# Low parts of the attention weights: accumulating DMAs in place of GpSimd's subtractions

## The chip, the cores and the metric

The kernel runs on one core of a Trainium2 chip. A core has engines that run their own instruction queues side by side: TensorE (in the profile PE for matmuls, PEld for weight loads), VectorE (DVE), ScalarE (ACT), GpSimd (POOL) and SyncE (SP, which here only issues DMAs). GpSimd can issue DMAs too, and only those of its queue add to what lies at their destination in this kernel. The metric is the device time of one launch in microseconds, as the median of the runs.

## The reference

Two layers of an encoder for 512 tokens with 1024 channels, in float32. Cut to what matters:

```python
for l in range(DEPTH):                       # 2
    h = rms_norm(x, ln1_g[l])
    proj = h @ w_in[l]                       # split: A's q, k, v; B's q, k, v; C's ranks; gate logits
    y_a = gqa_axial(...)                     # attention A: 8 query heads, 2 key heads
    y_b = diff_attention(...)                # attention B: 8 heads, difference of two softmaxes
    y_c = mla(...)                           # attention C: 8 heads from low-rank latents
    y = stack([y_a, y_b, y_c])
    merged = sum(sigmoid(gate_logits) * (y @ w_branch[l]), over the three)
    x = x + merged @ w_out[l]
    x = x + square(relu(rms_norm(x, ln2_g[l]) @ w_ff1[l])) @ w_ff2[l]
return rms_norm(x, final_g)
```

The kernel multiplies in float32r, a type to which its casts round. To keep the accuracy, each operand is split into a high part (the value rounded to float32r) and a low part (the value minus the high part), and a product is made of three: high by high, high by low, low by high.

## The kernel before

The kernel is written for a tile scheduler: the program lists the operations, and the scheduler makes each engine's order from the order of the list, the data each operation needs, and when a buffer comes free. A list of items, each with a cost in microseconds of TensorE, is the plan (`plan`, from line 1020 on). `run` (line 167) walks it. Before each item it does what has come due: weights whose item starts within `AHEAD_F` are fetched (a DMA of SP's queue into a buffer `wr`), weights whose item starts within `AHEAD_S` are split (`get`, line 55). So these two numbers set where in the list a weight's operations stand.

A weight is a `Weight` (line 43): 128 partitions by 256 to 1024 columns. `get` writes the high part `wh` with ScalarE (line 61, a cast) and the low part `wl` with a subtraction (line 67). There are two buffers of `wr` (`NWR`) and three each of `wh` and `wl` (`NW`). A cast waits until the matmuls of the weight three before have ended, and a fetch until the weight two before has been read for the last time, which is the end of the subtraction.

The subtraction is made by VectorE in one piece, or by GpSimd in pieces of 256 columns. `nw` counts the weights, and of each five those with `nw % 5 < POOLW` go to GpSimd. `POOLW` is `P0` = 1 at a layer's start (its projections), `PA` = 5 from the first attention to the last gates, so that all go to GpSimd there, and `PF` = 0 after that (output projection and MLP). The marked places are lines 1029, 1052, 1066 and 1130.

The order of a layer: keys and values of A, queries of A, parts of B's projections; then attention A woven with the rest of B's projections; attention B woven with gate matmuls (`gate_branch`, line 976) and C's projections; attention C woven with gates and C's per-pair projections; the last gates and branches; the output projection; the MLP. An attention item (`probs`, line 588) makes scores in PSUM (`sc`), their row maximum with VectorE (line 594), the exponential with ScalarE (line 599), the normalised rows with VectorE (lines 604 and, for B, 754 to 756); later the transposes (`pT`, line 610), the copies out of PSUM by ScalarE and VectorE (lines 613, 614) and the products with the values (`pv`).

The MLP's second product multiplies by sums of weight blocks (`Blocks`, line 72). Some of these sums are made by DMAs of GpSimd's queue that add one block onto another (lines 95 and 96). They are not changed.

Of the kernel before, what the change touches and what calls it, by code (L numbers as in the profile page):

```python
# [10 lines left out]
F32 = mybir.dt.float32  # L11
F32R = mybir.dt.float32r
I32 = mybir.dt.int32
AF = mybir.ActivationFunctionType
ALU = mybir.AluOpType
# [27 lines left out]
class Weight:  # L43
# [11 lines left out]
    def get(self):  # L55
        if self.parts is None:
            self.fetch()
            t = self.t
            wh = t.p.tile([128, self.cols], F32R, tag="wh", name="wh", bufs=t.NW)
            wl = t.p.tile([128, self.cols], F32R, tag="wl", name="wl", bufs=t.NW)  # L60
            t.nc.scalar.copy(wh, self.raw)  # L61
            t.nw += 1

            e, n = (t.nc.gpsimd, 256) if t.nw % 5 < t.POOLW else (t.nc.vector, 1024)
            for o in range(0, self.cols, n):
                q = slice(o, min(o + n, self.cols))
                e.tensor_tensor(wl[:, q], self.raw[:, q], wh[:, q].bitcast(F32), op=ALU.subtract)  # L67
            self.parts = wh, wl
        return self.parts

# [71 lines left out]
class Trunk:  # L142
# [24 lines left out]
    def run(self, plan):  # L167

        at, ws = 0.0, []
        for c, _, w in plan:  # L170
            ws += [(at - getattr(x, "lead", 0.0), x) for x in w]
            at += c
        ws.sort(key=lambda x: x[0])
        t0, kf, kg = self.t, 0, 0
        for c, f, _ in plan:
            now = self.t - t0
            while kf < len(ws) and ws[kf][0] <= now + self.AHEAD_F:
                ws[kf][1].fetch()
                kf += 1
            while kg < len(ws) and ws[kg][0] <= now + self.AHEAD_S:  # L180
                ws[kg][1].get()
                kg += 1
            self.tick(self.t)
            f()
            self.t += c

    @staticmethod
    def weave(att, fill):

        tf = sum(x[0] for x in fill)  # L190
        done, k, r = 0.0, 0, []
        for i, a in enumerate(att):
            r.append(a)
            while k < len(fill) and done + fill[k][0] / 2 <= tf * (i + 1) / len(att):
                r.append(fill[k])
                done += fill[k][0]
                k += 1
        return r + fill[k:]
# [821 lines left out]
    def plan(self, l):  # L1020
        nc = self.nc

        def begin():
            self.aG, self.aK, self.aR, self.ys = {}, {}, {}, {"a": {}, "b": {}, "c": {}}
            self.bz = {}
            self.bf, self.bs, self.bV = {"q": {}, "k": {}}, {"q": {}, "k": {}}, {}
            self.cQ, self.cK, self.cV, self.qr, self.mg, self.cf, self.mp, self.gc = {}, {}, {}, {}, {}, {}, {}, {}
            self.layer_consts(l)
            self.POOLW = self.P0
            self.hold = []  # L1030

        def stat():
# [13 lines left out]
        weave = self.weave  # L1046
        kv = self.a_kv(l)
        r = [(0, begin, [])] + kv + [(0, stat, [])] + self.a_q(l, 0) + self.a_q(l, 1)
        fb = self.b_qk(l, "q", 0) + self.b_qk(l, "k", 0) + self.b_v(l, 0)
        fb1 = self.b_qk(l, "q", 1) + self.b_qk(l, "k", 1) + self.b_v(l, 1)  # L1050
        r += fb[: self.FB]
        r += [(0, lambda: setattr(self, "POOLW", self.PA), [])]
        r += weave(self.att_a(), fb[self.FB :] + fb1)
        gb = [[self.gate_branch(l, n, d) for d in range(8)] for n in range(3)]
        att = self.att_b(l)
# [5 lines left out]
        g2 = [x[0] for x in gb[2]]  # L1061
# [1 line left out]
        r += weave(att[8:16], self.c_pair(l, 2) + self.c_v(l, 1) + gates(1, 4, 8))  # L1063
        r += weave(att[16:24], self.c_pair(l, 3) + g2[:3])
        r += weave(att[24:], g2[3:6])
        r += [(0, lambda: setattr(self, "POOLW", self.PF), [])] + g2[6:]
        r += [(0, self.tick, [])] + [x[1] for x in gb[2]]
        xs, x2, st2, ff = [], [], {}, []

# [57 lines left out]
                hs[p] += [h[:, :, 0:256], h[:, :, 256:512]]  # L1127

        def stat2():
            self.POOLW = self.PF  # L1130
            v = self.stat_var(self.stat_join(st2))
            self.r2 = self.p.tile([128, 4], F32, tag="rstd", name="r2", bufs=1)
            self.rsqrt(self.r2, v, 4)
# [71 lines left out]
        for c, n in enumerate(CHUNKS):  # L1205
            for j in range(2 * n):
                w = self.big(l, P_FF1 + j0 + j)
                if c and j < 2:
                    w.tag = "pt"
                r.append((cost, lambda j=j, w=w: ff1(j, w), [w]))  # L1210
                if c == 0 and j < 2:
                    r.append((0, rbc2 if j else stat2, []))
            j0 += 2 * n
            for m in range(4):
                blocks = Blocks(self, self.ff2_blocks(l, c, m), n)
                f = {i: Factor(blocks, i, 3.0 if m == 0 else 1.5) for i in range(1, 8)}
                order = [(i, (0, n)) for i in (1, 4, 2, 6, 5, 7, 3)]
                if m == 0:

                    e = n - 2  # L1220
                    order = [(1, (0, n))] + [(i, (0, e)) for i in (2, 4, 5)] + [(i, (e, n)) for i in (2, 4)]
                    order += [(6, (0, n)), (5, (e, n)), (7, (0, n)), (3, (0, n))]
                if c + 1 == len(CHUNKS) and l + 1 == self.depth and m == 3:
                    order = [(i, (0, n)) for i in (1, 4, 2, 6, 7, 5, 3)]
                for i, part in order:
                    r.append(((part[1] - part[0]) * 0.36, lambda c=c, m=m, i=i, w=f[i], part=part: ff2(c, m, i, w, part), [f[i]]))
# [12 lines left out]
    def go(self):  # L1239
        tc, nc = self.tc, self.nc  # L1240
        self.t, self.due, self.hold, self.nb, self.nw = 0.0, [], None, 0, 0

        self.NS4, self.NWR, self.NW, self.NTMP, self.NP = 25, 2, 3, 4, 4
        self.BANKS = {"S": 2, "T": 2, "V": 1, "L": 3}

        self.AHEAD_F, self.AHEAD_S = 8.0, 3.0
        self.LAG_T, self.LAG_V, self.LAG_C = 5.5, 6.0, 9.0
        self.LAG_Q, self.LAG_KV, self.LAG_R = 14.0, 14.0, 60.0

        self.P0, self.PA, self.PF = 1, 5, 0  # L1250
        self.FB = 16
        self.TAGQ = "ST"
        self.POOLW = self.P0
        with tc.tile_pool(name="c", bufs=1) as self.c, tc.tile_pool(name="p", bufs=1) as self.p, \
                tc.tile_pool(name="pp", bufs=1, space=bass.MemoryType.PSUM) as self.pp, \
                tc.tile_pool(name="pd", bufs=1, space=bass.MemoryType.DRAM) as pd:
            self.xd = pd.tile([128, 8, 512], F32, name="xd") if self.depth > 1 else None
            self.st, self.xg, self.xs = {}, [None] * 8, []
            plan = sum((self.plan(l) for l in range(self.depth)), [])
            self.setup()  # L1260
            self.g = self.c.tile([128, self.a["gains"].shape[1]], F32, name="g")
            nc.sync.dma_start(self.g, self.a["gains"])
            for d in range(8):
                if d % 2 == 0:
                    x = self.s4("x", dtype=F32)
                nc.sync.dma_start(x[:, d % 2], self.a["xT"][:, d])
                self.xs.append(x[:, d % 2])
                if d in (0, 4):
                    plan[1 + 3 * (d // 4)][2][0].fetch()
            self.tables()  # L1270
            for d in range(8):
                self.first_norm(0, d)
                if d in (0, 4):
                    plan[1 + 3 * (d // 4)][2][0].get()
            for d in range(8):
                self.stat_add(self.st, d, self.xs[d])
            self.run(plan)
# [108 lines left out]
```

## Time and profile before

| what | value |
|---|---|
| median of 3 runs (lowest, highest) | 1873.94 us (1873.64, 1875.34) |
| the profiled execution | 1873.65 us, its span 1871.9 us |
| TensorE busy | 1820.1 us, 97% |
| VectorE busy | 1382.5 us, 74% |
| ScalarE busy | 1010.6 us, 54% |
| GpSimd busy | 473.8 us, 25% |
| GpSimd's low parts (line 67) | 402 pieces, 296.4 us |
| granted TensorE clock | 0.994 |

The span runs from the first to the last instruction of the profiled execution. A group of instructions is told as line, engine, operation, what it writes and reads, and how many; then its busy time, the mean duration of one in ns, the idle time of the engine just before them, and what ended most of it. A row of the waits is who waited, for whom, us in total, times, and the longest. A row of the timeline is start, duration, engine, line, operation, and in brackets the idle time before it. The attentions fill about 75 to 525 us in the first layer and 985 to 1465 us in the second.

### The profile page before, as it was taken

To read this page: it belongs to the slowest core of one execution; us is meant where nothing else is said; L and a number is where in the kernel's file an instruction comes from. 1 tells how busy PE (TensorE), PEld (TensorE's weight loads), DVE (VectorE), ACT (ScalarE), POOL (GpSimd) and SP (SyncE) were. 2 spreads that over 40 slices of the span, in tenths; PEclk is the share of its full clock that TensorE was granted. 3 is DMA by queue.
4 is the path that set the end of the run, shared out by engine and by line. 5 is a ranking of instruction groups with operands and counts; after the bars stand their busy time and mean duration, and the time that the engine had idled before them with its cause. 6 is when DMAs were issued, how large, how long until landed. Compare 5 with 4: busy or idle time off the path is not lost.

```text
span 1871.9 us, 30054 instructions
## 1 busy us (share of the span) xinstructions
PE 1820.1 (97%) x10960; PEld 1601.4 (86%) x10960; DVE 1382.5 (74%) x2815; ACT 1010.6 (54%) x1852; POOL 473.8 (25%) x622
## 2 busy tenths in 40 slices
PE   8999999999999999999999999999999999999997
PEld 8998878777888898988999988788878888989897
DVE  8788889755665776767887888796566667777677
ACT  5577666655544544444545766665554444444443
POOL 4321443454101110101243224434540001001011
PEclk9999999999999999999999999999999999999998
DMA  5213341332143373645632134313232525637353
GB/s 163 69 51 86 96 108 48 96 84 81 51 169 101 93 184 103 155 130 133 153 104 64 41 101 113 93 49 89 81 93 65 166 90 118 168 95 183 106 145 95
DMA packets 85059, 197.26 MB, mean 105 GB/s; under 512 B 11952, under 2 KB 28720, under 8 KB 84912
## 3 DMA queue, kind: packets, MB, share of 16 engines
q1 hardware_dynamic: 74544, 178.56, 31.9%
q0 software_dynamic: 10368, 16.78, 6.0%
q8 instruction: 87, 1.43, 0.3%
q14 instruction: 60, 0.49, 0.1%
HBM read 174.32 MB, written 4.19 MB: 95 GB/s over the span
## 4 chain that ended last, share of the span: by engine, by line
PE 74%; DVE 11%; DMA 6%; ACT 5%; issue 2%; POOL 1%; SPq 0%; DVEq 0%; ACTq 0%; POOLq 0%
PE ff L222 18%; PE ff L1162 13%; PE gate L222 12%; PE br L222 6%; PE tm L314 5%; PE out L222 4%; PE sc L222 4%; PE pv L222 4%; PE pT L610 3%; DMA fa<-wff 2%; DMA wr<-w 2%; PE c_rank L222 2%; DVE mx L594 1%; DVE p L756 1%; DVE fl L116 1%
## 5 line engine op out<-in xcount | busy, mean ns | idle before, releaser
L67 POOL TENSOR_TENSOR wl<-wr,wh 128x256 fp32r<-128x256 f32 (+1 forms) x402 | 296.4, 766 | 533.2 <-ACT wh L61 512.0
L61 ACT CAST wh<-wr 128x1024 fp32r<-128x1024 f32 (+5 forms) x246 | 224.6, 914 | 343.8 <-PE ff L222 113.7
L1162 PE MATMUL ff<-h,fh 128*128 128x256 f32 x1792 | 324.4, 283 | 2.1 <-DVE x L1170 1.8
L222 PE MATMUL ff<-xg,wh 128*128 128x512 f32 x1024 | 315.8, 390 | 0.0
L1162 PEld LDWEIGHTS ff<-h,fh 128*128 128x128 f32 x1792 | 279.0, 192 | 4.2 <-issue 2.5
L1162 PE MATMUL ff<-h,fl 128*128 128x256 f32 x896 | 254.2, 285 | 1.9 <-DVE fl L116 1.8
L222 PE MATMUL gate<-xg,wh 128*128 128x512 f32 x768 | 241.9, 393 | 1.1 <-DVE c_K L230 1.1
L222 PEld LDWEIGHTS ff<-xg,wh 128*128 128x128 f32 x1024 | 191.7, 188 | 39.5
L115 ACT CAST fh<-fa 128x640 fp32r<-128x640 f32 (+1 forms) x144 | 108.8, 762 | 177.8 <-PE ff L1162 100.0
L314 PE MATMUL tm<-wh,xg 128*128 128x256 f32 x1024 | 203.4, 290 | 0.0
L594 DVE TENSOR_REDUCE mx<-sc 128x1 f32<-128x512 f32 x256 | 173.8, 683 | 38.4 <-PE sc L222 37.4
L222 PE MATMUL ff<-xg,wl 128*128 128x512 f32 x512 | 199.2, 389 | 0.0
L1162 PEld LDWEIGHTS ff<-h,fl 128*128 128x128 f32 x896 | 171.1, 192 | 5.3 <-DVE fl L116 4.8
L222 PEld LDWEIGHTS gate<-xg,wh 128*128 128x128 f32 x768 | 142.9, 188 | 29.9 <-PE pv L222 1.4
L314 PEld LDWEIGHTS tm<-wh,xg 128*128 128x128 f32 x1024 | 165.6, 193 | 0.2
L116 DVE TENSOR_TENSOR fl<-fa,fh 128x640 fp32r<-128x640 f32 (+1 forms) x144 | 126.3, 881 | 36.9 <-ACT fh L115 33.9
L67 DVE TENSOR_TENSOR wl<-wr,wh 128x1024 fp32r<-128x1024 f32 (+3 forms) x117 | 134.1, 1146 | 25.8 <-ACT wh L61 25.8
L222 PE MATMUL gate<-xg,wl 128*128 128x512 f32 x384 | 150.6, 392 | 0.0
L613 ACT CAST pt<-pT 128x512 fp32r<-128x512 f32 x192 | 111.8, 585 | 65.0 <-PE pT L610 62.9
L314 PE MATMUL tm<-wl,xg 128*128 128x256 f32 x512 | 145.7, 285 | 0.0
L614 DVE TENSOR_TENSOR pt<-pT,pt 128x512 fp32r<-128x512 f32 x192 | 131.3, 686 | 19.3 <-ACT pt L613 17.7
L96 POOL DMA_DIRECT2D fa<-wff x24 | 21.5, 896 | 421.8 <-DMA fa<-wff 302.4
(253 smaller groups left out, 3610.4 us busy)
## 6 DMA issues: line engine op xcount, KB each, us to landing
wr<-w SPq DMA_DIRECT2D x170, 512.0 KB, 3.6
fa<-wff SPq DMA_DIRECT2D x64, 320.0 KB, 3.5
wr<-w SPq DMA_DIRECT2D x52, 256.0 KB, 2.9
fa<-wff SPq DMA_DIRECT2D x32, 384.0 KB, 3.8
b_sq<-b_f SPq DMA_DIRECT2D x96, 64.0 KB, 2.9
b_sk<-b_f SPq DMA_DIRECT2D x96, 64.0 KB, 2.0
fa<-wff POOLq DMA_DIRECT2D x16, 320.0 KB, 4.8
fs<-wff SPq DMA_DIRECT2D x32, 160.0 KB, 2.7
```

The source lines that it names most:

```text
L61: t.nc.scalar.copy(wh, self.raw)
L67: e.tensor_tensor(wl[:, q], self.raw[:, q], wh[:, q].bitcast(F32), op=ALU.subtract)
L96: t.nc.gpsimd.dma_start(r["21"], self.src[0], accum_op=ALU.add)
L115: t.nc.scalar.copy(a, x)
L116: t.nc.vector.tensor_tensor(b, x, a.bitcast(F32), op=ALU.subtract)
L222: self.nc.tensor.matmul(out, l, r, start=(i == 0), stop=(i == n - 1))
L314: self.nc.tensor.matmul(ps, l, r, start=(u == 0 and i == 0 and tt % 2 == 0), stop=(u == 1 and tt % 2 == 1 and i == len(p) - 1))
L594: nc.vector.tensor_reduce(m, s, axis=AX.X, op=ALU.max, negate=True)
L610: nc.tensor.transpose(T[:, k], p[:, k * 128 : (k + 1) * 128], self.ident)
L613: nc.scalar.copy(h[:, :, q], T)
L614: nc.vector.tensor_tensor(lo[:, :, q], T, h[:, :, q].bitcast(F32), op=ALU.subtract)
L1162: nc.tensor.matmul(bk[tag], x, y, start=(new and a == 0), stop=(part[1] == n and a == len(pairs) - 1), skip_group_check=True)
```

## The change

For a weight that GpSimd split, ScalarE now writes two tiles: the high part as before, and minus the high part, into the low part's buffer. Then a DMA on GpSimd's queue reads the weight from HBM once more and adds it there, so that the low part stands in the buffer when the DMA has landed. VectorE's subtraction is no longer cut at 1024 columns; no weight is wider than that. The variable is renamed to `DMAW`, with the same values at the same places. While it isn't zero, weights are split 6.0 ahead (`AHEAD_D`) and not 3.0; fetches are made 10.0 ahead and not 8.0, everywhere.

```diff
             t.nc.scalar.copy(wh, self.raw)
             t.nw += 1
-            e, n = (t.nc.gpsimd, 256) if t.nw % 5 < t.POOLW else (t.nc.vector, 1024)
-            for o in range(0, self.cols, n):
-                q = slice(o, min(o + n, self.cols))
-                e.tensor_tensor(wl[:, q], self.raw[:, q], wh[:, q].bitcast(F32), op=ALU.subtract)
+            if t.nw % 5 < t.DMAW:
+                t.nc.scalar.activation(wl, self.raw, AF.Copy, scale=-1.0)
+                t.nc.gpsimd.dma_start(wl, self.src, accum_op=ALU.add)
+            else:
+                t.nc.vector.tensor_tensor(wl, self.raw, wh.bitcast(F32), op=ALU.subtract)
             self.parts = wh, wl
...
-            while kg < len(ws) and ws[kg][0] <= now + self.AHEAD_S:
+            while kg < len(ws) and ws[kg][0] <= now + (self.AHEAD_D if self.DMAW else self.AHEAD_S):
                 ws[kg][1].get()
...
-        self.AHEAD_F, self.AHEAD_S = 8.0, 3.0
+        self.AHEAD_F, self.AHEAD_S, self.AHEAD_D = 10.0, 3.0, 6.0
...
-        self.POOLW = self.P0
+        self.DMAW = self.P0
```

More of the change, by code (lines that the diff above doesn't have):

```diff
@@ L1051, in plan @@
         r += fb[: self.FB]
-        r += [(0, lambda: setattr(self, "POOLW", self.PA), [])]
+        r += [(0, lambda: setattr(self, "DMAW", self.PA), [])]
         r += weave(self.att_a(), fb[self.FB :] + fb1)
@@ L1065, in plan @@
         r += weave(att[24:], g2[3:6])
-        r += [(0, lambda: setattr(self, "POOLW", self.PF), [])] + g2[6:]
+        r += [(0, lambda: setattr(self, "DMAW", self.PF), [])] + g2[6:]
         r += [(0, self.tick, [])] + [x[1] for x in gb[2]]
@@ L1129, in stat2 @@
         def stat2():
-            self.POOLW = self.PF
+            self.DMAW = self.PF
             v = self.stat_var(self.stat_join(st2))
@@ L1252, in go @@
         self.TAGQ = "ST"
-        self.POOLW = self.P0
+        self.DMAW = self.P0
         with tc.tile_pool(name="c", bufs=1) as self.c, tc.tile_pool(name="p", bufs=1) as self.p, \
```

## Prediction

> **What bounds the kernel now.** I read the first page from the top: span, busy times, then the chain that ended last.
>
> ```profile
> span 1871.9 us, 30054 instructions
> PE 1820.1 (97%) x10960; PEld 1601.4 (86%) x10960; DVE 1382.5 (74%) x2815; ACT 1010.6 (54%) x1852; POOL 473.8 (25%) x622
> ...
> PE 74%; DVE 11%; DMA 6%; ACT 5%; issue 2%; POOL 1%; SPq 0%; DVEq 0%; ACTq 0%; POOLq 0%
> ```
>
> TensorE is busy for 97% of the span, and GpSimd, whose work the change takes away, makes 1% of the chain. Next come the two stretches of the attentions, one in each layer (busy times by window; the columns are the stretch, then PE, PEld, DVE, ACT, POOL with their counts, clock, DMA share and GB/s).
>
> ```profile
> 75.00:525.00 450.00, 438.81 (x2555) 374.57 (x2554) 338.12 (x762) 283.35 (x581) 159.18 (x216) 1.00 0.28 77
> 985.00:1465.00 480.00, 467.17 (x2721) 399.68 (x2721) 363.77 (x809) 297.90 (x604) 163.69 (x222) 1.00 0.28 80
> ```
>
> Here TensorE is idle for 450.00 - 438.81 = 11.2 us and 480.00 - 467.17 = 12.8 us. These 24.0 us are nearly all that any change to the helpers of the attentions can win, about 1.3% of the span. VectorE is at 75%, ScalarE at 63%.
>
> Who is waited for in them? First, the low part's own line over the whole span (who waited for line 67), then TensorE's longest waits in the first stretch.
>
> ```profile
> who waited for it (us, times):
> ...
>   PEld tm L327: 0.3, 1
>   PEld tm L314: 0.2, 1
> ```
>
> ```profile
> PE pT L610 <- DVE p L604: 3.2, 3, 2.7
> ```
>
> ```profile
> PEld sc L222 <- ACT p L599: 7.1, 17, 1.6
> ```
>
> TensorE waited 0.5 us in all for a low part. What it waits for in the attentions is the softmax: ScalarE's exponential (a score bank comes free) and VectorE's normalised rows. So making the low parts sooner is worth nothing by itself; the change can win only through VectorE and ScalarE, and lose by late low parts.
>
> **What is removed.** GpSimd's subtractions, and with them their hold on VectorE.
>
> ```profile
> L67 POOL TENSOR_TENSOR wl<-wr,wh 128x256 fp32r<-128x256 f32 (+1 forms) x402 | 296.4, 766 | 533.2 <-ACT wh L61 512.0
> L61 ACT CAST wh<-wr 128x1024 fp32r<-128x1024 f32 (+5 forms) x246 | 224.6, 914 | 343.8 <-PE ff L222 113.7
> ...
> L67 DVE TENSOR_TENSOR wl<-wr,wh 128x1024 fp32r<-128x1024 f32 (+3 forms) x117 | 134.1, 1146 | 25.8 <-ACT wh L61 25.8
> ```
>
> There are 246 high parts and 117 low parts on VectorE, so GpSimd makes 129, in 402 pieces of 296.4 us. GpSimd is on no path here, so those us are free; what counts is VectorE beside it. The trace has one plain case (in order of time), and then the two rows of line 756 (least, median and greatest ns; then busy us and mean ns):
>
> ```profile
> 231.41 0.15 DVE L254 TENSOR_TENSOR rst<-rst,rsh 128x8 f32<-128x8 f32 x1
> ...
> 231.84 1.32 DVE L756 SCALAR_TENSOR_TENSOR p<-p,z 128x512 f32<-128x512 f32 x1
> ...
> 231.88 4.65 POOL L67 TENSOR_TENSOR wl<-wr,wh 128x256 fp32r<-128x256 f32 x6 [6.41 <-ACT wh L61]
> ...
> 233.09 0.71 DVE L256 TENSOR_TENSOR rst<-rsy 128x8 f32<-128x8 f32 x1
> ...
> 236.65 0.50 PE L222 MATMUL sc<-b_sk,b_sq 96*128 96x512 f32 x1 [1.17 <-ACT p L599]
> ```
>
> ```profile
> L756 DVE SCALAR_TENSOR_TENSOR p<-p,z x64: 734/752/1323, 179.8 to 1260.3; 128x512 f32<-128x512 f32 x64
> ```
>
> ```profile
> L756 DVE SCALAR_TENSOR_TENSOR p<-p,z 128x512 f32<-128x512 f32 x64 | 55.3, 864 | 0.9
> ```
>
> While GpSimd runs its six pieces, an operation of 0.15 us takes 0.71 and line 756 takes 1.32; TensorE then waits 1.17 us. Line 756 has a median of 752 ns and a mean of 864, so its 64 instructions lose 64 x 0.112 = 7.2 us of VectorE, half of it in each layer. How much of this is on the path? The least is nothing, the most is the 24.0 us of idle time; the one wait of 1.17 us is shown, others are likelier small. I take 3 us a layer, **-6 us**, with 0 and -15 as bounds (no reason lets all idle time go, since the waits for ScalarE stay).
>
> **What is added on ScalarE.** 129 passes that write minus the high part. The trace has no such pass; the nearest row is the cast of the same tile on the same engine, in the first stretch:
>
> ```profile
> L61 ACT CAST wh<-wr 128x1024 fp32r<-128x1024 f32 (+3 forms) x65 | 54.0, 833 | 65.2 <-PE gate L222 29.6 <-issue 18.6 <-DMA wr<-w 10.6
> ```
>
> 129 x 0.833 = 107 us, about 54 a layer, which lifts ScalarE in the first stretch from 283 to 337 of 450 us, 75%. Behind each pass on ScalarE's queue stand the exponentials and the copies of the transposed probabilities, and TensorE waits for these. If its 7.1 us of waits for the exponential grow with the load (337/283), that is +1.3 us a layer; where a pass of 1.05 us falls just ahead of a wait, it is added whole. One such place is known:
>
> ```profile
> 461.36 0.41 PE L610 MATMUL pT<-ident,p 128*128 128x128 f32 x2 [2.69 <-DVE p L604]
> ```
>
> Together 2 us a layer, **+4 us**. Bounds: 0 (ScalarE has 167 us of idle time there), and +17, if each of the 17 waits becomes 0.5 us longer in both layers.
>
> **What is moved: the low part's landing.** It now needs the second pass, then a DMA of GpSimd's queue that reads the weight again and adds. The trace has such DMAs in the MLP:
>
> ```profile
> q1 hardware_dynamic: 74544, 178.56, 31.9%
> q0 software_dynamic: 10368, 16.78, 6.0%
> ...
> wr<-w SPq DMA_DIRECT2D x170, 512.0 KB, 3.6
> ...
> fs<-wff POOLq DMA_DIRECT2D x32, 160.0 KB, 4.5
> fa<-wff POOLq DMA_DIRECT2D x8, 384.0 KB, 5.0
> ```
>
> From 160 to 384 KB the time from issue to landing grows by 0.5 us, so I estimate 5.3 us for 512 KB, the issue itself included. From the end of the cast to the low part: 1.05 + 5.3 = 6.35 us, where GpSimd needs four pieces of 0.766 = 3.1. So each is 3.3 us later. Does TensorE notice? Four weights in order of time: the cast, GpSimd's pieces, the first matmul that reads the low part.
>
> ```profile
> 23.81 1.05 ACT L61 CAST wh<-wr 128x1024 fp32r<-128x1024 f32 x1 [1.63 <-DMA wr<-w]
> ...
> 29.02 0.28 PE L314 MATMUL tm<-wl,xg 128*128 128x256 f32 x1
> ```
>
> ```profile
> 186.50 1.05 ACT L61 CAST wh<-wr 128x1024 fp32r<-128x1024 f32 x1
> ...
> 197.65 0.40 PE L222 MATMUL gate<-xg,wl 128*128 128x512 f32 x1
> ```
>
> ```profile
> 340.63 1.05 ACT L61 CAST wh<-wr 128x1024 fp32r<-128x1024 f32 x1
> ...
> 341.76 4.27 POOL L67 TENSOR_TENSOR wl<-wr,wh 128x256 fp32r<-128x256 f32 x6 [5.30 <-ACT wh L61]
> ...
> 345.25 0.39 PE L222 MATMUL gate<-xg,wl 128*128 128x512 f32 x1
> ```
>
> ```profile
> 364.25 0.73 POOL L67 TENSOR_TENSOR wl<-wr,wh 128x256 fp32r<-128x256 f32 x1 [8.48 <-ACT wh L61]
> ...
> 368.75 0.39 PE L222 MATMUL gate<-xg,wl 128*128 128x512 f32 x1
> ```
>
> The cast at 186.50 is the usual case: it ends at 187.55, the new low part lands at 193.9, and the matmul comes at 197.65, so 3.7 us are left. The tight ones: 341.68 + 6.35 = 348.0 against 345.25, 2.8 us late; 364.2 (GpSimd starts right behind the cast) + 6.35 = 370.5 against 368.75, 1.8 late; 24.86 + 6.35 = 31.2 against 29.02, 2.2 late. With the first two in each layer: 2 x 4.6 + 2.2 = 11.4 us, if nothing else changes. Three things do. The weight's buffer comes free at the end of the second pass (342.7), not of GpSimd's fourth piece (344.6), so the fetch of the weight after next is issued 1.9 us earlier; SP's queue shows that it waits for just that:
>
> ```profile
> SPq L53 <- POOL wl L67: 299.2, 120, 8.4
> ```
>
> The longer lookahead (6.0 for 3.0) asks for a weight earlier, ahead of the attention's items on ScalarE. And the order of TensorE's matmuls is made anew by the scheduler, which puts other ready work ahead of a late part. I keep about a third, **+4 us**; bounds 0 and +23 (twice 11.4, if the landings take longer than in the MLP).
>
> Weighed against the Trainium skill: "DMA: Bandwidth & Descriptors", section "Anatomy of one DMA — SWDGE (gpsimd) path", fits such a DMA with about 2.0 us plus its bytes at 436 GB/s, and by it 512 KB would take 3.2 us, the low part would come only 1.2 us later than now, and this term would be about nothing (an estimate from that page). The rows of this trace, 4.5 us already for 160 KB, disagree, and the sum goes by them.
>
> **The rest.** What an issue costs GpSimd, from the MLP:
>
> ```profile
> L96 POOL DMA_DIRECT2D fa<-wff x24: 857/862/1426, 630.8 to 1839.0; - x24
> ```
>
> It issues 129 DMAs at some 0.86 us for 402 pieces, so its own queue gets shorter; the sums of squares and the merged branches that stand behind them wait no longer than now. The added traffic is 402 pieces of 128 KB, 52.7 MB. At the queue's price (6.0% of 1871.9 us for 16.78 MB, 6.7 us a MB) that is 353 us of all 16 engines, over 930 us: the share rises from 0.28 to 0.66. That is below full, and I cost it at nothing; if not, the second rival prices it. Fetching 10.0 ahead and not 8.0 finds SP's queue held by buffers as now: nothing, within 3 us either way.
>
> **Sum.** -6 + 4 + 4 = +2 us. The profiled execution took 1873.65 us (span 1871.9 and 1.75 around it); the median of the runs is 1873.94, 0.3 above, so the forecast is 1875.7 for such an execution and **1876 us** for a median.
>
> **Rivals.**
> *Relief wins.* VectorE's free port shortens the softmax enough to remove half of the 24.0 us of idle time, and the late parts are hidden: 1874 - 12 + 2 = 1864. For it: the 1.17 us case, and VectorE at 75%. Against: only 7.2 us of line 756 is lost to it.
> *The low parts come late (slower).* One mechanism: accumulating DMAs at a share of 0.66 land as the slowest of the MLP do, 9.1 us in the row below, not 5.3. It decides once a landing takes over 9 us: then the tight weights are late by 6.6, 5.6 and 6.0, so 2 x 12.2 + 6.0 = 30 us; with two thirds of it real, 1894.
>
> ```profile
> DMA to landing us min/median/max: 3.2/4.6/9.1
> ```
>
> The Trainium skill has a rule that would drive this: "SBUF — State Buffer", section "SBUF: two separate sides", says that VectorE's two-port operations keep GpSimd from writing descriptors; no run shows yet what it does here.
> *ScalarE becomes the bound.* The +17 us of its upper bound, less 3 of relief: 1888. For it: 75% load with the exponentials behind; against: 113 us of idle time left.
> *The lookahead alone pays.* Weights asked for earlier remove a third of the idle time, the rest cancels: 1866.
>
> **How the numbers follow.** Forecast (1870 to 1881) 0.40, relief 0.25, ScalarE 0.17, late parts 0.10, lookahead 0.08. Faster, the same and slower are parted at 0.2% (3.7 us), about what a measurement of this kernel can tell. Of the forecast's 0.40 I give 0.04 to faster, 0.24 to the same, 0.12 to slower. Faster: 0.04 + 0.25 + 0.08 = 0.37; slower: 0.12 + 0.17 + 0.10 = 0.39; the same 0.24. The range is 1861 to 1893; it leaves out the ends of relief and of late parts.
>
> **What will show it.** GpSimd's busy time falls by about 185 us (296 less 129 x 0.86); ScalarE's rises by 107; line 756's mean falls from 864 to about 752; issue to landing of the new DMAs at 5.3 us; TensorE's waits for low parts under 5 us a layer. I am wrong if these DMAs land in 4 us or in 8, if ScalarE's exponentials take over TensorE's waits, or if the two stretches' idle time moves by more than 10 us.

## The result and the profile after

| what | before | after |
|---|---|---|
| median of 4 runs (lowest, highest) | 1873.79 us (1871.38, 1875.34) | 1928.20 us (1922.73, 1932.96) |
| ratio, 95% interval | | 1.0292 (1.0276 to 1.0307) |
| the profiled execution, its span | 1873.65, 1871.9 us | 1932.96, 1931.2 us |
| granted TensorE clock | 0.994 | 0.979 |

The change makes the kernel 2.9% slower, where 2 us more had been forecast; 1928 lies 35 us above the upper end of the range. The changed kernel has one line more above most of the functions: line 222 is now 223, line 756 is 757, and so on; line 65 is the new ScalarE pass and line 66 the new DMA.

The first page of the changed kernel: span, busy times, queues, the chain that ended last.

```profile
span 1931.2 us, 29908 instructions
PE 1844.8 (96%) x10960; PEld 1618.8 (84%) x10960; DVE 1348.3 (70%) x2813; ACT 1101.0 (57%) x1983; POOL 288.3 (15%) x351
...
q0 software_dynamic: 29232, 69.92, 22.0%
...
PE 76%; DMA 9%; issue 5%; ACT 5%; DVE 4%; POOL 0%; SPq 0%; ACTq 0%; DVEq 0%; POOLq 0%
```

Of the 59.3 us by which the span grew, 24.7 are TensorE's busy time (1844.8 - 1820.1), with the same 10960 matmuls, and 34.6 its idle time. VectorE is busy for 34 us less and has nearly left the chain (11% to 4%); DMAs grew in it (6% to 9%). The two stretches of the attentions (columns as in the prediction):

```profile
75.00:525.00 450.00, 421.04 (x2409) 358.32 (x2408) 310.09 (x728) 312.21 (x619) 74.22 (x89) 0.97 0.58 129
985.00:1465.00 480.00, 452.95 (x2700) 391.09 (x2699) 338.25 (x800) 327.75 (x651) 87.23 (x110) 0.97 0.57 127
```

Idle time went from 11.2 to 29.0 us in the first and from 12.8 to 27.1 in the second, and the clock, 1.00 in both before, is 0.97. (The stretches are fixed times; as the changed kernel runs behind by up to 59 us, they hold somewhat less of its work.) TensorE's waits (who waited for whom, us, times, longest) say for what:

```profile
PE gate L223 <- DMA wl<-w: 39.9, 14, 5.2
...
PE tm L223 <- DMA wl<-w: 5.0, 2, 2.9
PE tm L315 <- DMA wl<-w: 4.5, 1, 4.5
...
PE tm L328 <- DMA wl<-wkv: 3.4, 1, 3.4
PE uk L223 <- DMA wl<-w: 3.3, 2, 1.7
```

20 waits of 56.1 us together for the low parts' DMAs, where there had been 0.5 us for low parts. The waits for the softmax, which had been the largest of the attentions, have nearly gone (before, then after):

```profile
PE pT L610 <- DVE p L604: 5.7, 5, 2.7
...
PE sc L222 <- ACT p L599: 3.7, 4, 1.2
```

```profile
PE pT L611 <- DVE p L605: 1.0, 2, 0.5
...
PE sc L223 <- ACT p L600: 0.2, 1, 0.2
```

The DMAs themselves, issue to landing in us (DMA issues by size), and what SP's queue waits for ahead of a weight's fetch:

```profile
wr<-w SPq DMA_DIRECT2D x170, 512.0 KB, 3.9
wl<-w POOLq DMA_DIRECT2D x76, 512.0 KB, 7.1
...
wl<-w POOLq DMA_DIRECT2D x36, 256.0 KB, 5.0
...
wl<-w POOLq DMA_DIRECT2D x8, 128.0 KB, 4.0
```

```profile
SPq L53 <- ACT wl L65: 444.5, 90, 13.6
```

A low part of 512 KB lands 7.1 us after its issue, in the median. The last row suggests a cause of part of it, which no run tested by itself: the event that lets the accumulating DMA go, the end of the ScalarE pass, is also the one that lets the fetch of the weight after next go, since that pass is now the last reader of the raw weight. So the two transfers start side by side. The longest wait for a low part, in order of time (start, duration, engine, line):

```profile
245.21 1.08 ACT L65 ACTIVATE wl<-wr 128x1024 fp32r<-128x1024 f32 x1
...
246.31 9.82 SPq L53 DMA_DIRECT2D wr<-w  x3
...
246.58 0.86 POOL L66 DMA_DIRECT2D wl<-w  x1 [7.73 <-ACT wl L65]
...
247.93 0.86 POOL L66 DMA_DIRECT2D wl<-w  x1 [0.49 <-ACT wl L65]
...
257.04 0.80 PE L223 MATMUL gate<-xg,wl 128*128 128x512 f32 x1 [5.20 <-DMA wl<-w]
257.63 1.06 PE L223 MATMUL gate<-xg,wh 128*128 128x512 f32 x2
...
262.33 0.63 PE L223 MATMUL gate<-xg,wl 128*128 128x512 f32 x1
262.75 0.85 PE L223 MATMUL gate<-xg,wh 128*128 128x512 f32 x2
263.44 0.39 PE L223 MATMUL gate<-xg,wl 128*128 128x512 f32 x1
```

The pass ends at 246.29. A fetch goes at 246.31, the first of three, the gate's accumulating DMA at 246.58 and that of the next weight at 247.93; the gate's lands 10.4 us after its issue. Behind the wait of 5.20 us the same matmul takes 0.63 us until 262.33, and 0.39 from 263.44 on. That is the second part of the loss, and the granted clock shows it. Fifteen of the twenty waits last 2 us or more. The windows of 6.1 us behind them follow (the column after POOL is the clock). The first eleven are the gates' waits, of 2.00, 2.40, 2.41, 2.82, 3.19, 3.54, 3.60, 3.70, 4.09, 4.82 and 5.20 us in this order; the last four are those of the time-major products (`tm`), of 2.10, 2.87, 3.41 and 4.48 us:

```profile
1328.60:1334.70 6.10, 6.10 (x25) 5.06 (x26) 1.17 (x3) 0.74 (x2) 0.00 (x0) 0.75 0.25 49
211.90:218.00 6.10, 6.07 (x20) 4.83 (x21) 1.19 (x3) 0.16 (x2) 0.00 (x0) 0.72 1.03 217
1437.20:1443.30 6.10, 6.07 (x20) 4.86 (x21) 2.23 (x5) 4.62 (x8) 0.86 (x1) 0.72 0.68 166
485.70:491.80 6.10, 6.10 (x21) 4.96 (x22) 1.85 (x4) 4.19 (x6) 0.86 (x1) 0.77 0.72 150
1165.60:1171.70 6.10, 6.10 (x15) 4.82 (x16) 0.81 (x2) 0.00 (x0) 0.00 (x0) 0.54 0.99 212
1313.10:1319.20 6.10, 6.09 (x22) 4.96 (x23) 2.63 (x5) 4.55 (x9) 0.68 (x1) 0.72 0.20 74
360.50:366.60 6.10, 6.10 (x18) 4.92 (x19) 2.50 (x5) 3.31 (x7) 0.00 (x0) 0.58 0.24 72
1210.10:1216.20 6.10, 6.06 (x16) 4.76 (x17) 0.00 (x0) 0.28 (x1) 1.82 (x2) 0.55 0.82 175
1346.20:1352.30 6.10, 6.10 (x15) 4.82 (x16) 0.00 (x0) 0.00 (x0) 0.00 (x0) 0.52 0.68 136
393.40:399.50 6.10, 6.05 (x21) 4.93 (x22) 0.00 (x0) 0.00 (x0) 0.00 (x0) 0.76 0.49 99
257.00:263.10 6.10, 6.06 (x14) 4.84 (x15) 0.00 (x0) 0.00 (x0) 0.89 (x1) 0.50 0.71 170
...
1376.80:1382.90 6.10, 5.52 (x32) 4.25 (x32) 3.94 (x8) 4.40 (x10) 0.43 (x1) 1.00 0.80 187
423.40:429.50 6.10, 5.96 (x29) 5.18 (x29) 2.51 (x5) 2.59 (x6) 0.00 (x0) 0.72 0.80 180
970.60:976.70 6.10, 6.08 (x25) 6.08 (x26) 1.22 (x1) 1.04 (x1) 1.03 (x3) 0.51 0.33 126
33.60:39.70 6.10, 6.10 (x35) 6.10 (x36) 5.32 (x18) 0.29 (x1) 1.63 (x4) 0.64 0.32 101
```

One minus the clock, summed over the fifteen, is 5.00; times 6.1 us that is 30.5 us. TensorE's busy time is 24.7 us above that of the kernel before, and 31.3 us above that of the kernel without these DMAs (1813.5 us, below), which has none of these waits. So the lower clock behind the waits accounts for nearly all of the slower matmuls.

### The profile page after: what moved, and what is told of

Its sections match the earlier page's. It is cut to its first block, busy times and chain, and to the rows that moved or that the text cites. A ratio compares the mean times of both kernels' runs of the same rounds, so it can differ in the third digit from the quotient of the medians.

```text
span 1931.2 us, 29908 instructions
## 1 busy us (share of the span) xinstructions
PE 1844.8 (96%) x10960; PEld 1618.8 (84%) x10960; DVE 1348.3 (70%) x2813; ACT 1101.0 (57%) x1983; POOL 288.3 (15%) x351
## 3 DMA queue, kind: packets, MB, share of 16 engines
q1 hardware_dynamic: 74544, 178.56, 30.5%
q0 software_dynamic: 29232, 69.92, 22.0%
## 4 chain that ended last, share of the span: by engine, by line
PE 76%; DMA 9%; issue 5%; ACT 5%; DVE 4%; POOL 0%; SPq 0%; ACTq 0%; DVEq 0%; POOLq 0%
PE ff L223 18%; PE ff L1163 13%; PE gate L223 12%; PE tm L315 7%; DMA wl<-w 6%; PE br L223 5%; PE out L223 5%; PE sc L223 4%; PE pv L223 3%; PE pT L611 3%; PE c_rank L223 3%; DMA fa<-wff 2%; ACT p L600 1%; ACT wl L65 1%; PE tp L344 1%
## 5 line engine op out<-in xcount | busy, mean ns | idle before, releaser
L223 PE MATMUL gate<-xg,wh 128*128 128x512 f32 x768 | 257.2, 413 | 0.0
L66 POOL DMA_DIRECT2D wl<-w x130 | 112.6, 866 | 729.5 <-ACT wl L65 563.0
L223 PE MATMUL gate<-xg,wl 128*128 128x512 f32 x384 | 161.4, 420 | 39.9 <-DMA wl<-w 39.9
L223 PEld LDWEIGHTS gate<-xg,wh 128*128 128x128 f32 x768 | 153.7, 202 | 31.8
L615 DVE TENSOR_TENSOR pt<-pT,pt 128x512 fp32r<-128x512 f32 x192 | 131.0, 686 | 26.9 <-ACT pt L614 24.5
L223 PEld LDWEIGHTS gate<-xg,wl 128*128 128x128 f32 x384 | 77.7, 202 | 61.1 <-DMA wl<-w 44.9
```

Of the source, the lines that this page charges most:

```text
L66: t.nc.gpsimd.dma_start(wl, self.src, accum_op=ALU.add)
L223: self.nc.tensor.matmul(out, l, r, start=(i == 0), stop=(i == n - 1))
L615: nc.vector.tensor_tensor(lo[:, :, q], T, h[:, :, q].bitcast(F32), op=ALU.subtract)
```

## The experiments

Theory L: the loss is TensorE waiting for low parts that the accumulating DMAs land too late, with slower matmuls behind each wait. Rivals: A, the ScalarE passes; P, the new order from the longer lookahead; T, the added traffic; M, matmuls slowed by the DMAs' writes. Ratios are to runs of the kernel before on the same chip, with 95% intervals. The sum of TensorE's waits for DMAs of low parts is called W.

**The lookahead alone**, on the kernel before, and the changed kernel without it:

```diff
-        self.AHEAD_F, self.AHEAD_S = 8.0, 3.0
+        self.AHEAD_F, self.AHEAD_S, self.AHEAD_D = 10.0, 3.0, 6.0
...
-            while kg < len(ws) and ws[kg][0] <= now + self.AHEAD_S:
+            while kg < len(ws) and ws[kg][0] <= now + (self.AHEAD_D if self.POOLW else self.AHEAD_S):
```

> The kernel before with the changed kernel's lookahead alone: AHEAD_F 10 in place of 8 everywhere, and the casts looked at 6 us ahead in place of 3 wherever GpSimd has a share. GpSimd still makes the low parts. Theory L (the loss is the wait for low parts that the accumulating DMAs land too late): no DMA, no loss, 1868 to 1880 us. Rival P (the longer lookahead re-plans the engines' order, and the new order is the loss): 1905 to 1930 us. Rival A (the 129 added ScalarE passes are the loss): 1868 to 1880 us, as L.

Measured: 1873.94 us, ratio 1.0010 (1.0000 to 1.0019).

```diff
-        self.AHEAD_F, self.AHEAD_S, self.AHEAD_D = 10.0, 3.0, 6.0
+        self.AHEAD_F, self.AHEAD_S, self.AHEAD_D = 8.0, 3.0, 3.0
```

> The changed kernel with the lookahead of before (8 and 3 us): the accumulating DMAs stay, and their casts may be planned up to 3 us later. L: no better than the changed kernel, 1925 to 1950 us, with TensorE's waits for low parts at 56 us or more. P: back to 1870 to 1885 us. A: unchanged, 1920 to 1935 us.

Measured: 1923.96 us, ratio 1.0285 (1.0257 to 1.0312), W 49.5 us. The lookahead neither costs nor saves anything that shows. P falls. L's guess that the shorter one would make it worse was not borne out either; probably casts and fetches wait for buffers, so that 3 us more of lookahead send no DMA earlier.

**Without the DMAs**:

```diff
                 t.nc.scalar.activation(wl, self.raw, AF.Copy, scale=-1.0)
-                t.nc.gpsimd.dma_start(wl, self.src, accum_op=ALU.add)
```

> The changed kernel without the accumulating DMAs alone: ScalarE still makes the second pass, and the low part stays minus the rounded weight, so the products of the low parts are left wrong in value but take the same time on TensorE. L: the whole loss goes and the relief of VectorE is left, 1860 to 1875 us. A: the ScalarE passes are still there, so 1915 to 1930 us. P: the lookahead is still there, so 1905 to 1930 us.

Measured: 1853.44 us, ratio 0.9900 (0.9881 to 0.9919). With the passes and the lookahead left in, leaving out the DMAs takes away 75 us, more than the whole loss; A falls. The low parts are incomplete here, so this is a probe and no version to use. The first page of this kernel, and its gate matmuls beside those of the changed kernel (busy us, mean ns):

```profile
PE 1813.5 (98%) x10960; PEld 1596.7 (86%) x10960; DVE 1347.4 (73%) x2813; ACT 1099.9 (59%) x1983; POOL 177.4 (10%) x220
...
L222 PE MATMUL gate<-xg,wl 128*128 128x512 f32 x384 | 150.7, 392 | 0.0
```

```profile
L223 PE MATMUL gate<-xg,wl 128*128 128x512 f32 x384 | 161.4, 420 | 39.9 <-DMA wl<-w 39.9
```

The other finding of this run is the gain: 18 us below the kernel before, so the relief is real. VectorE's busy time fell by 35.1 us (1382.5 to 1347.4). 2.6 us of that are two low parts fewer: with the longer lookahead VectorE makes 115 and not 117, and 131 weights and not 129 have the second pass; the rest is the same operations taking less time. TensorE's waits for VectorE's and ScalarE's softmax rows (`p`) fell with it, from 5.7 to 0.4 us and from 3.7 to 2.3, and those for two operands of attention A that VectorE makes (`a_G`, `a_kr`) from 8.5 to 1.1.

**The ScalarE pass alone**, on the kernel before:

```diff
+            if t.nw % 5 < t.POOLW:
+                t.nc.scalar.activation(wl, self.raw, AF.Copy, scale=-1.0)
             e, n = (t.nc.gpsimd, 256) if t.nw % 5 < t.POOLW else (t.nc.vector, 1024)
```

> The kernel before with the added ScalarE pass alone: where GpSimd makes the low part, ScalarE first writes minus the weight into the low part's buffer, and GpSimd's subtraction then writes over it. GpSimd starts about 1.1 us later. L: 1874 to 1884 us (ScalarE's 107 us more lie beside other work). A: 1905 to 1930 us. P: 1870 to 1880 us.

Measured: 1881.68 us, ratio 1.0051 (1.0034 to 1.0068). That is 9.9 us more, in which GpSimd's start one pass later is contained, so the pass by itself costs at most about that in this kernel.

**The traffic alone**, first held by nothing:

```diff
-                t.nc.gpsimd.dma_start(wl, self.src, accum_op=ALU.add)
+                wd = t.pd.tile([128, self.cols + 16], F32, tag="wd", name="wd", bufs=4)
+                t.nc.gpsimd.dma_start(wd[:, 0 : self.cols], self.src, accum_op=ALU.add)
...
+            self.pd = pd
```

> The changed kernel with its accumulating DMAs of the same bytes, from the same queue, sent into a scratch buffer in HBM in place of the low part: the transfers and GpSimd's issues stay, and nothing waits for them (the low part stays minus the rounded weight, so the products of the low parts are left wrong in value). Theory L (the loss is TensorE waiting for landings): as without the DMAs, 1850 to 1862 us. Rival T (the 52.7 MB of traffic, or the writing of its descriptors, is what costs: late fetches, slower VectorE): 1885 to 1930 us.

Measured: 1908.15 us, ratio 1.0199 (1.0184 to 1.0214), in T's range and not in L's. But the DMA row of its page, which in the changed kernel shows 4 to 6 tenths over the first layer's attentions, shows that this was another load:

```profile
DMA  8999999232214255463652123313231534637353
```

With nothing to wait for, the transfers of both layers ran in the first seven slices of the span, about 330 us, at 220 to 250 GB/s; from 330 us on TensorE was busy for 1547.0 of 1570 us at a clock of 1.00. So the run prices DMA engines that are full, which they are not in the changed kernel. So again, paced as in the changed kernel:

```diff
-                t.nc.gpsimd.dma_start(wl, self.src, accum_op=ALU.add)
+                wd = t.pd.tile([128, self.cols + 16], F32, tag="wd", name="wd", bufs=4)
+                t.nc.gpsimd.dma_start(wd[:, 0 : self.cols], wl.bitcast(F32), accum_op=ALU.add)
...
+            self.pd = pd
```

> The traffic again, paced: the changed kernel with each accumulating DMA sent, after the second ScalarE pass as in the changed kernel, from the low part's buffer into a scratch buffer in HBM (same bytes, same queue, same moment; TensorE reads the low part without waiting for it, and it stays minus the rounded weight, wrong in value). In the traffic run before this the transfers, held by nothing, all ran in the first 330 us at 220 to 250 GB/s, so its 1908 us prices saturated DMA engines and not these. Theory L (waiting for landings is the loss): 1853 to 1865 us. Rival T (traffic): 1900 us or more.

Measured: 1854.96 us, ratio 0.9914 (0.9900 to 0.9929): as without DMAs. Its rows (DMA issues; first stretch):

```profile
wd<-wl POOLq DMA_DIRECT2D x76, 512.0 KB, 7.0
```

```profile
75.00:525.00 450.00, 443.25 (x2582) 378.62 (x2581) 330.27 (x770) 328.32 (x648) 74.49 (x89) 1.00 0.62 136
```

The same landings at about the same share of the DMA engines (0.62, and 0.58 in the changed kernel), with nobody waiting, cost 1.5 us over the kernel without DMAs, which is within the intervals. T falls. (These DMAs read the low part's buffer and write HBM; the changed kernel's read HBM and write the buffer.)

**Smaller or earlier DMAs.** All three on the changed kernel: a quarter of the columns (the rest of the low part is left incomplete), two halves, and the same DMA sent before the cast:

```diff
-                t.nc.gpsimd.dma_start(wl, self.src, accum_op=ALU.add)
+                n = self.cols // 4
+                t.nc.gpsimd.dma_start(wl[:, 0:n], self.src[:, 0:n], accum_op=ALU.add)
```

> The changed kernel with the accumulating DMA over the first quarter of the columns alone (128 KB in place of 512 KB; the other three quarters of the low part stay minus the rounded weight, wrong in value). 128 KB landed in 4.0 us in the changed kernel's trace against 7.1 us for 512 KB, so a low part is there 3.1 us sooner. L: of the 56 us of waits, each shortened by 3.1 us, about 8 us stay, and of the 75 us that leaving the DMAs out gave (1928 to 1853) about 11: 1858 to 1868 us. T: a quarter of the bytes, so a quarter of the 75 us, 1869 to 1880 us; if the count of DMAs and issues is what costs and not their bytes, 1900 us or more.

Measured: 1866.11 us, ratio 0.9967 (0.9951 to 0.9983), in L's range, with W at 13.7 us and not 8.

```diff
-                t.nc.gpsimd.dma_start(wl, self.src, accum_op=ALU.add)
+                n = self.cols // 2
+                for q in (slice(0, n), slice(n, self.cols)):
+                    t.nc.gpsimd.dma_start(wl[:, q], self.src[:, q], accum_op=ALU.add)
```

> The changed kernel with each accumulating DMA in two halves of the columns. 256 KB landed in 5.0 us in its trace, so the first half is there about 2.1 us sooner, and the second is wanted 12 matmuls later. L: of the 56 us of waits some 19 stay when each is 2.1 us shorter: 1853 + 75 x 19/56 = 1878, range 1868 to 1895 us. T: the bytes are the same and the issues twice as many, 1925 us or more.

Measured: 1893.38 us, ratio 1.0121 (1.0106 to 1.0136), W 25.5 us. In the range, but at its upper end: two halves in flight together land in 6.1 us each, not 5.0.

```diff
-            t.nc.scalar.copy(wh, self.raw)
             t.nw += 1
-            if t.nw % 5 < t.DMAW:
-
+            d = t.nw % 5 < t.DMAW
+            if d:
                 t.nc.scalar.activation(wl, self.raw, AF.Copy, scale=-1.0)
                 t.nc.gpsimd.dma_start(wl, self.src, accum_op=ALU.add)
-            else:
+            t.nc.scalar.copy(wh, self.raw)
+            if not d:
```

> The changed kernel with its two ScalarE passes in the other order: minus the weight first, then the cast, so that each accumulating DMA of the same size is sent the 0.9 us of the cast earlier. Theory L (the loss is the waits, and the slower matmuls follow the waits): 24 waits, each 0.9 us shorter, take 56 us to about 36, and TensorE's busy time falls with them: 1928 - 75 x 20/56 = 1901, range 1893 to 1912 us. Rival M (the matmuls are slower because the accumulating DMAs write while TensorE reads): the busy time stays at 1840 us or more, 1908 to 1925 us.

Measured: 1894.61 us (1884.62 to 1900.87), ratio 1.0101 (1.0054 to 1.0148), W 34.1 us in 18 waits, TensorE busy 1831.2 us. Sending the DMA one pass of ScalarE earlier gives 34 us back (the four executions spread over 16 us, so that is rough). The landing of 512 KB fell too, from 7.1 to 6.3 us. SP's queue (line 66 is the cast here, line 64 the pass) now waits more often for the cast that follows the DMA's release than for the pass that makes it:

```profile
SPq L53 <- ACT wh L66: 364.2, 65, 13.2
...
SPq L53 <- ACT wl L64: 192.5, 40, 9.4
```

That fits two transfers colliding, but no run varied that alone. M falls: with equal bytes and equal sizes the busy time goes down by 13.6 us together with W, and in the changed kernel the clock behind the waits already accounts for 30.5 of the 31.3 us.

**Asking for the low part later.** The products of a stationary weight are ordered all high, then all low:

```diff
-            r += [(wh[:, sl], x[:, 0]), (wh[:, sl], x[:, 1]), (wl[:, sl], x[:, 0])]
+            r += [(wh[:, sl], x[:, 0]), (wh[:, sl], x[:, 1])]
+        for k, x in enumerate(xs):
+            r += [(wl[:, off + k * 128 : off + (k + 1) * 128], x[:, 0])]
```

> The changed kernel with another order of a projection's products where the weight is the stationary side (gates, branches, output, up-projections): all products of the high part first, then all of the low part. A gate's first low product then comes 16 matmuls in, not 2, which is 14 x 0.39 = 5.5 us later; what is computed is the same. L: the gates' and the up-projections' waits (43 us of the 56) go, the time-major ones (about 13 us) stay: 1853 + 75 x 13/56 = 1870, range 1860 to 1882 us. T: 1915 us or more.

Measured: 1889.64 us, ratio 1.0097 (1.0069 to 1.0125), W 24.5 us; better than the changed kernel by 39 us, but above the range of L. The control, the same edit in the kernel before, shows why the gain is smaller:

> The kernel before with that same order of products, as a control: TensorE waited 0.5 us for low parts in the kernel before, so both theories expect 1866 to 1877 us.

Measured: 1885.77 us, ratio 1.0079 (1.0064 to 1.0094). The order itself costs about 15 us in the kernel before, which neither theory had; TensorE's waits for the exponential, 3.7 us there, are 12.0 us with it, and why was not looked into. With this order the change costs 4 us, not 54.

The kernels with these DMAs and the usual order of products, VectorE making none of these low parts, together ("excess" is the median less the 1853.4 us without DMAs; W and the busy time are of one execution each):

| kernel | W, us | TensorE busy, us | median, us | excess, us |
|---|---|---|---|---|
| no DMA | 0 | 1813.5 | 1853.4 | 0 |
| quarter | 13.7 | 1817.1 | 1866.1 | 12.7 |
| halves | 25.5 | 1828.0 | 1893.4 | 40.0 |
| DMA first | 34.1 | 1831.2 | 1894.6 | 41.2 |
| lookahead 8, 3 | 49.5 | 1846.9 | 1924.0 | 70.6 |
| the changed kernel | 56.1 | 1844.8 | 1928.2 | 74.8 |

The excess is 0.9 to 1.6 times W, 1.33 in the changed kernel: except for the shortest waits (the quarter), each us waited costs more than itself, by the slower matmuls behind it.

**Keeping the relief without the waits.** VectorE makes the first half, which is wanted first, and the DMA the second:

```diff
-                t.nc.scalar.activation(wl, self.raw, AF.Copy, scale=-1.0)
-                t.nc.gpsimd.dma_start(wl, self.src, accum_op=ALU.add)
+                n = self.cols // 2
+                t.nc.scalar.activation(wl[:, n:], self.raw[:, n:], AF.Copy, scale=-1.0)
+                t.nc.gpsimd.dma_start(wl[:, n:], self.src[:, n:], accum_op=ALU.add)
+                t.nc.vector.tensor_tensor(wl[:, 0:n], self.raw[:, 0:n], wh[:, 0:n].bitcast(F32), op=ALU.subtract)
```

> The changed kernel with the first half of each such low part made by VectorE's subtraction and the second half by a DMA onto minus the high part (256 KB). VectorE makes the half that is wanted first; the DMA's half is wanted 12 matmuls (4.7 us) later and lands in about 5.0 us. L: the waits for low parts almost all go; VectorE has 129 x 0.6 = 77 us more than in the changed kernel, still less than before with GpSimd on its side: 1855 to 1872 us. T: half the bytes, so half the loss, 1885 us or more.

Measured: 1867.49 us, ratio 0.9974 (0.9963 to 0.9985), W 10.1 us (the 8.6 us in the next expectation leave out two of the waits). And, against this version, with the DMA's half ahead of the cast:

```diff
-            t.nc.scalar.copy(wh, self.raw)
...
                 t.nc.scalar.activation(wl[:, n:], self.raw[:, n:], AF.Copy, scale=-1.0)
                 t.nc.gpsimd.dma_start(wl[:, n:], self.src[:, n:], accum_op=ALU.add)
+            t.nc.scalar.copy(wh, self.raw)
```

> The half-and-half version (VectorE the first half of the low part, the accumulating DMA the second) with minus the weight's second half written ahead of the cast: the DMA is sent 0.9 us earlier, VectorE's half starts 0.6 us later. 8.6 us of waits for low parts were left there, most under 1 us over: L expects about half to go, 1860 to 1867 us.

Measured: 1863.78 us, ratio 0.9953 (0.9938 to 0.9969), W 1.3 us, the 256 KB landing in 4.2 us (4.7 in the version before it). It is the fastest kernel here whose low parts are complete, faster than both. With a quarter for VectorE in place of the half, against this version:

```diff
-                n = self.cols // 2
+                n = self.cols // 4
```

> The same with VectorE making a quarter and the DMA three quarters (384 KB, about 6.0 us by the line through 4.0, 5.0 and 7.1): VectorE has some 39 us less than with a half, but the DMA's first column is wanted 6 matmuls (2.3 us) after VectorE's, not 12. L: waits between those of the half (8.6 us) and of the whole (56 us), 1862 to 1885 us.

Measured: 1868.00 us, ratio 0.9974 (0.9964 to 0.9985), W 9.2 us. 384 KB landed in 5.3 us, not in the 6.0 of a line through 4.0, 5.0 and 7.1: the landing is not a matter of size alone.

**All low parts on VectorE** (the changed kernel), and VectorE and GpSimd half each (the kernel before):

```diff
-        self.P0, self.PA, self.PF = 1, 5, 0
+        self.P0, self.PA, self.PF = 0, 0, 0
```

> The changed kernel with every low part made by VectorE: no GpSimd, no added ScalarE pass, no DMA. VectorE gets 129 x 1.14 = 147 us more than in the changed kernel. If the relief of VectorE is what makes the kernel without the DMAs 18 us faster than before, it is used up here: 1865 to 1890 us. If it is that GpSimd stands out of VectorE's way, some of it stays: 1853 to 1865 us.

Measured: 1869.19 us, ratio 0.9980 (0.9970 to 0.9989). The gain of the kernel without DMAs is nearly used up, as the first of the two cases had it, with VectorE busy for 102 us more than in the changed kernel and not 147; 3 to 4 us below the kernel before are left.

```diff
-            e, n = (t.nc.gpsimd, 256) if t.nw % 5 < t.POOLW else (t.nc.vector, 1024)
-            for o in range(0, self.cols, n):
-                q = slice(o, min(o + n, self.cols))
+            h = self.cols // 2 if t.nw % 5 < t.POOLW else self.cols
+            for e, i, j, n in ((t.nc.vector, 0, h, h), (t.nc.gpsimd, h, self.cols, 256)):
+              for o in range(i, j, n):
+                q = slice(o, min(o + n, j))
                 e.tensor_tensor(wl[:, q], self.raw[:, q], wh[:, q].bitcast(F32), op=ALU.subtract)
```

> The kernel before with VectorE making the first half of each such low part and GpSimd the second half in two pieces: no DMA, no added ScalarE pass, GpSimd with half the work it had. If it is GpSimd's work beside VectorE and the buffers held by its slow pieces that cost the 18 us, half of it comes back, less VectorE's 77 us: 1862 to 1872 us.

Measured: 1885.21 us, ratio 1.0069 (1.0053 to 1.0085); the expectation was wrong by its sign. Three first-page rows tell a part of why: half with a DMA, half with GpSimd, all on VectorE.

```profile
PE 1819.9 (98%) x10960; PEld 1601.9 (86%) x10960; DVE 1408.7 (75%) x2944; ACT 1061.9 (57%) x1983; POOL 293.4 (16%) x351
```

```profile
PE 1826.0 (97%) x10960; PEld 1604.6 (85%) x10960; DVE 1435.9 (76%) x2944; ACT 1011.6 (54%) x1852; POOL 361.1 (19%) x426
```

```profile
PE 1822.2 (97%) x10960; PEld 1603.2 (86%) x10960; DVE 1450.1 (78%) x2944; ACT 1013.4 (54%) x1852; POOL 186.8 (10%) x220
```

The same 2944 VectorE operations, of the same sizes but for two weights, take 27.2 us longer with GpSimd's pieces beside them than with DMAs. Making the other half of the low parts too costs VectorE only 14.2 us more than that, and the kernel with all on VectorE is 16 us faster. Here half of GpSimd's work did not give half of the relief. As the faster of the two has the busier VectorE, VectorE's load can't be the whole reason; what else GpSimd's pieces held up was not separated.

## Why the prediction was wrong

**The cap and who waits for whom: right.** No kernel won more than the 24 us of idle time, and the softmax's waits fell with the relief, though those for A's operands, which the prediction had not named, fell by more (8.5 to 1.1 us).

**The relief of VectorE: right in mechanism, too small.** -6 us in the sum, -15 as the bound. Line 756 went to a mean of 748 ns, as its median of 752 had told, but it is one line of many: over all of them VectorE's operations took about 32 us less, not 7.2. Without the DMAs the kernel gains 18 us with the ScalarE passes already paid. How much of that is VectorE's time, and how much the buffers that come free earlier when no slow piece reads them, was not separated.

**ScalarE: right.** +4, bounds 0 and +17; with the pass alone the kernel before took 9.9 more. Busy time rose by 90 us, not 107. ScalarE did not become the bound.

**The landing: the step that failed, in three places.**

First its size. 5.3 us was drawn from rows of 160 and 384 KB in the MLP, which differ by 0.5 us; in the attentions 128, 256 and 512 KB took 4.0, 5.0 and 7.1 in the median. What the landing depends on besides the size stays open: two DMAs of 384 KB took 5.0 in this same kernel, and 256 KB took from 4.2 to 6.1 us over the runs, which differ in what was in flight beside them and in when they were sent. From the end of the cast to the low part it is then 1.06 (the pass) + 0.29 + 7.1 = 8.4 us, 5.3 later than before and not 3.3, so that of the usual weight's 3.7 us only 1.7 are left and a DMA that lands somewhat late is waited for. Not five waits (two in each layer and one more) but twenty were the outcome.

Second the "third" that I kept: none of the three things that were to soften it shows. The weight's buffer comes free with the event that sends the DMA, so the fetch runs beside it, which may have harmed; the longer lookahead moved nothing (the first two runs); and the waits stand at the same products in both layers, where the new order has no other work ahead of the late part.

Third, what had no term at all: behind a wait TensorE runs slower for up to about 6 us, which makes 24.7 us against the kernel before and 31.3 against the one without DMAs. The term was +4 with +23 as its bound, and measured 75. Of the signs of being wrong that it named, landings of 4 us or of 8 would not have told, as 7.1 lies between them; the idle time of the two stretches, up by 17.8 and 14.3 us, did.

The Trainium skill's fit in "DMA: Bandwidth & Descriptors", section "Anatomy of one DMA — SWDGE (gpsimd) path", about 2.0 us plus bytes at 436 GB/s, which the prediction had set aside, was further off: 3.2 us for 512 KB (an estimate from that page) against the 7.1 measured.

**Traffic and issues at nothing: right.** Queue 0 moved 69.92 MB, 53 more, as worked out; the share of the DMA engines in the attentions was 0.58, not 0.66; the paced run prices it at 1.5 us, within the noise. GpSimd's busy time fell by 185.5 us, as told.

**The rivals.** "The low parts come late" was the case, at a chance of 0.10, but with a wrong point and price: I had it decide from landings of 9 us and cost 1894; it decided at 7.1 and cost 1928, for the reasons above. Its driver, VectorE keeping GpSimd from writing descriptors ("SBUF — State Buffer", section "SBUF: two separate sides", of the Trainium skill), does not show in the issues: one took 0.87 us in the mean, and the MLP's of line 96 took 0.90 before. Whether it is part of the landing is open. "Relief wins" (1864) priced the relief too low: without the DMAs the kernel takes 1853. That the half-and-half version measures 1863.78 is chance, as VectorE there makes half of these low parts too. "The lookahead alone pays" and "ScalarE becomes the bound" were no case.

## What to carry to other kernels

Moving work to a DMA moves its result by the DMA's whole latency, so price that by the largest transfer of the stretch where it will run, next to the transfers that start with it, and compare it with the slack of each consumer one by one; here the scheduler's order put nothing else ahead of the twenty late parts. Count the slower matmuls behind a wait too: the loss here was 0.9 to 1.6 times the time waited, 1.33 in the changed kernel. A part of what is gained by relieving an engine (9 of 18 us here) can be kept by splitting the work so that the part wanted first is made at once and only the part wanted last takes the slow way.

## What the runs showed of the hardware

The clock. In the changed kernel the granted clock stayed at 1.00 behind a wait of 1.64 us (the first row below). Behind five of the six waits of 2.0 to 2.9 us it was 0.72 to 0.77 over the next 6.1 us, but 1.00 behind the one of 2.10; behind the nine of 3.2 to 5.2 it was 0.50 to 0.64 seven times, and 0.72 and 0.76. The length of the wait doesn't decide alone: in the run with the DMA ahead of the cast, the clock was 0.72 behind a wait of 1.81 us (at 1312 us) and 1.00 behind one of 2.48 (at 1344 us). The waits needn't be for these DMAs: in the run whose transfers saturated the DMA engines nobody waited for a low part, and its first 150 us, with 24 us of idle time, had a clock of 0.91 (the second fence).

```profile
376.50:382.60 6.10, 6.08 (x30) 4.92 (x31) 2.63 (x5) 1.12 (x2) 0.00 (x0) 1.00 0.29 61
```

```profile
0.00:150.00 150.00, 125.84 (x917) 120.91 (x918) 102.38 (x242) 84.69 (x162) 72.25 (x101) 0.91 1.01 232
```

The Trainium skill, "TensorE: Matmul & The Clock Gate", section "Part 1: The HAM clock gate (the "warmup" mystery)", has the clock halved after an idle window of about 3.4 us and whole again after as long a busy one. The halving agrees (0.50 behind the wait of 5.20 us). The lengths agree in part: here waits of 2.0 to 2.9 us were mostly followed by a lower clock already, and it took about 6 us of matmuls to come back behind the longest; a mean of 0.72 over 6.1 us would be a halved clock for 3.4 us (an estimate from these rows).
